# Up projection of a gated FFN: ScalarE writes the first product into the bank that the later ones add onto, two bank sums a pair, four buffers for products that run ahead

## The chip, the cores and the metric

The kernel runs on one core of one Trainium2 chip. The metric is the device time of one execution in microseconds; lower is better. Five engines work side by side, each through its own queue in a fixed order: TensorE (PE), VectorE (DVE), ScalarE (ACT), GpSimd (POOL) and SyncE (SP), which here issues the DMA transfers. PE writes its sums into banks of 128 x 512 float32 in PSUM; the other engines read them from there.

## The reference

One decoder layer on 1024 positions of 1024 channels: layer norm, a mixing sublayer (a convolution branch and a state-space branch), and a gated feed-forward block (FFN), each with a residual and a layer norm. The change lies in the FFN:

```python
u, g = split(h @ w_ffn_up)              # 1024 x 1024 times 1024 x 5632
u, g = causal depthwise conv of 3 taps along the positions, plus bias
y = (u * silu(g)) @ w_ffn_down          # 1024 x 2816 times 2816 x 1024
h = layer_norm(alpha * h + y)
```

(The names are shortened; the convolution runs over both halves.)

## The kernel before, in words

**Matmuls.** Each float32 operand is split into two parts of a shorter format, a high part (a cast on ACT) and what is left of it (a subtraction on DVE). `mm3` makes one product of three matmuls, high x high, high x low and low x high (L165, L166, L167). A *product* in the FFN is four `mm3` steps, 12 matmuls of 128 x 512, into one bank.

**Up projection.** 22 steps j; each makes 128 channels of the value half (`uv`) and 128 of the gate half (`ug`) for all 1024 positions. Positions and channels are cut into 2 x 2 blocks, and a scheme of Strassen's kind makes a step of seven products instead of eight. The position blocks and their sums are ready ahead: b11, b21, b22, t1, t2, t3, t4. `up_first` (L805) makes two products, b11 and b11 + b21, in one bank of the pool `pacc`; ACT copies the bank out after each (L811, L815), and the copy goes to DRAM (`first_scr`). The first 8 steps' `up_first` run ahead; the other 14 are spread over the 22 steps. `up_rest` (L837) makes the five others: `up_weights` loads two raw weight blocks (`ra`, `rb`), makes their sums on DVE (L828 to L831) and splits them (`split_pair`: cast L730, subtraction L731); `s` and half of `ug` come back from `first_scr`; and the products t2, t1, t3, b22 and t4 go into three banks of the pool `psm`, which has four. DVE takes the sums from the banks (L853, L855, L857, L859, L861):

```python
product(pb, lambda i: w24[:, i, :HALF], bl["t2"], True)
V.tensor_tensor(out=s, in0=s, in1=pb, op=ALU.add)                 # L853
product(pd, lambda i: w10[:, i, :HALF], bl["t1"], True)
V.tensor_tensor(out=uv[:, late], in0=s, in1=pd, op=ALU.add)       # L855
```

The convolution follows: one ACT pass with the third tap (L867) and two DVE passes (L871) for each half, silu on ACT (L881) and the gate on DVE (L882), tile `fo`. Every second step then makes sums of the two steps' results for the down projection (L896 to L899) and stores them to DRAM (`b_scr`, `t_scr`).

**Down projection.** `down` (L903) makes seven products p of 11 steps k, each with its own sum of weights and of stored blocks. `load(p, k)` fetches both halves into a tile `dr`, makes sums where p needs them (L924 for p=4, with a second tile `do`), and splits the tile into `w_dn` (L990, L991). Raw tiles come in turn from `wst` and from `raw` of the up projection, three buffers each; `w_dn` comes from two pools of three. For p=0 and p=1 `load` also fetches the blocks c3 and c4 (tile `c`, L955 and L959), which later products need. c4 and the rows of the last layer norm (`ln_g`, `ln_b`) lie where the position blocks of the up projection lay.

**Order.** A scheduler orders each engine's instructions when the kernel is built; `tc.high_priority` lets a block's instructions go as far ahead as buffers and data allow. SP's queue holds all loads and stores in one line.

Of the kernel before, what the change touches and what calls it, by code (L numbers as in the profile page):

```python
# [8 lines left out]
F32 = mybir.dt.float32  # L9
F32R = mybir.dt.float32r  # L10
AF = mybir.ActivationFunctionType
ALU = mybir.AluOpType
# [4 lines left out]
P = 128  # L17
D = 1024
# [37 lines left out]
def kernel(  # L56
# [30 lines left out]
    def bank(which):  # L87
# [53 lines left out]
    b2_scr, t32_scr, t41_scr = (  # L141
        [dram.tile([P, T], F32, name=f"{n}_scr{k}") for k in range(NK)] for n in ("b2", "t32", "t41")
    )
    c_scr = [dram.tile([8, P, HALF], F32, name=f"c_scr{i}") for i in range(2)]
    g_scr = [dram.tile([8, P, HALF], F32, name=f"g_scr{i}") for i in range(2)]
# [659 lines left out]
    def up_first(qp, bl, j):  # L805

        w = weights(wup[2 * j], f"ue{j}")
        ps = bank(1)
        product(ps, lambda i: w[:, i, 0:HALF], bl["b11"], True)
        s1 = qp.tile([P, HALF], F32, tag="first", bufs=2, name=f"s1_{j}")  # L810
        A.copy(s1, ps)  # L811
        SY.dma_start(first_scr[j][0], s1)
        product(ps, lambda i: w[:, i, HALF:D], bl["b21"], False)
        c11 = qp.tile([P, HALF], F32, tag="first", bufs=2, name=f"c11_{j}")
        A.copy(c11, ps)  # L815
        SY.dma_start(first_scr[j][1], c11)

    def up_weights(upp, j):


        with tc.high_priority(offset=2000):
            r1 = upp.tile([P, D], F32, tag="raw", bufs=3, name=f"ra{j}")
            SY.dma_start(r1, wup[2 * j])
            r2 = upp.tile([P, D], F32, tag="raw", bufs=3, name=f"rb{j}")
# [3 lines left out]
            V.tensor_tensor(out=s3, in0=a11, in1=a21, op=ALU.add)  # L828
            V.tensor_tensor(out=a21, in0=a21, in1=a22, op=ALU.add)
            V.tensor_tensor(out=a11, in0=a21, in1=a11, op=ALU.add)  # L830
            V.tensor_tensor(out=a12, in0=a12, in1=a11, op=ALU.add)  # L831
            w24 = split_pair(wsp, r1, f"s24_{j}")
            w10 = split_pair(wsp, r2, f"s10_{j}")
            w3 = split_pair(upp, s3, f"s3_{j}", HALF, 2)
        return w24, w10, w3

    def up_rest(upp, bl, j, before):  # L837

        w24, w10, w3 = up_weights(upp, j)
        ug, uv = (
            upp.tile([P, T + 32], F32, tag="u", bufs=3, name=f"f{n}{j}") for n in ("ug", "uv")
        )
        s = upp.tile([P, HALF], F32, tag="s", bufs=2, name=f"s{j}")
        SY.dma_start(s, first_scr[j][0])
        SY.dma_start(ug[:, 2 : 2 + HALF], first_scr[j][1])
        G.memset(ug[:, :2], 0.0)
        G.memset(uv[:, :2], 0.0)
        pb, pc_, pd = bank(0), bank(0), bank(0)  # L850
        late = slice(2 + HALF, 2 + T)
        product(pb, lambda i: w24[:, i, :HALF], bl["t2"], True)
        V.tensor_tensor(out=s, in0=s, in1=pb, op=ALU.add)  # L853
        product(pd, lambda i: w10[:, i, :HALF], bl["t1"], True)
        V.tensor_tensor(out=uv[:, late], in0=s, in1=pd, op=ALU.add)  # L855
# [3 lines left out]
        V.tensor_tensor(out=ug[:, late], in0=s, in1=pd, op=ALU.add)  # L859
        product(pc_, lambda i: w10[:, i, HALF:], bl["t4"], False)  # L860
        V.tensor_tensor(out=uv[:, 2 : 2 + HALF], in0=pc_, in1=s, op=ALU.subtract)  # L861
        os = []
        j = j // 2 + j % 2 * NK
        for jj, u in ((j, ug), (NF + j, uv)):
            o = upp.tile([P, T], F32, tag="o", bufs=3, name=f"fo{jj}")
            wc = PC_FW + 3 * jj
            A.activation(  # L867
                out=o, in_=u[:, 2 : 2 + T], func=AF.Identity, scale=pc[:, wc + 2 : wc + 3]
            )
            for k in range(2):  # L870
                V.scalar_tensor_tensor(  # L871
                    out=o,
                    in0=u[:, k : k + T],
                    scalar=pc[:, wc + k : wc + k + 1],
                    in1=o,
                    op0=ALU.mult,
                    op1=ALU.add,
                )
# [20 lines left out]
        V.tensor_tensor(out=a[:, early], in0=b[:, early], in1=t[:, late], op=ALU.add)  # L899
        SY.dma_start(t32_scr[j - NK], t)  # L900
        SY.dma_start(t41_scr[j - NK], a)

    def down(upp, dp, g, b):  # L903

# [18 lines left out]
        def add(dst, x, y):  # L923
            V.tensor_tensor(out=dst, in0=x, in1=y, op=ALU.add)  # L924
# [3 lines left out]
        def raw(name):  # L928
            nonlocal n_raw
            n_raw += 1  # L930
            pl, tag = ((wst, "st"), (upp, "raw"))[n_raw % 2]
            return pl.tile([P, D], F32, tag=tag, bufs=3, name=f"{name}_{n_raw}")

        last = []

        def load(p, k):
# [5 lines left out]
                b2_scr[k][:, E],  # L942
                t32_scr[k][:, L],
                t32_scr[k][:, E],
                t41_scr[k][:, L],
                t41_scr[k][:, E],
                b2_scr[k][:, L],
            )[p]
            with tc.high_priority(offset=4000):
                st = raw("dr")  # L950
                w_st = st[:, E]
                SY.dma_start(st[:, L], x)
                if p == 0:
                    SY.dma_start(w_st, a11)
                    SY.dma_start(c3[k], a21)  # L955
                    add(c3[k], c3[k], w_st)
                elif p == 1:
                    SY.dma_start(w_st, a12)
                    SY.dma_start(c4[k], a22)  # L959
                    add(c4[k], c4[k], w_st)  # L960
                elif p == 2:
                    SY.dma_start(w_st, a22)
                    add(w_st, w_st, c3[k])
                elif p == 3:
                    w_st = c3[k]
                    add(c4[k], c4[k], c3[k])
                elif p == 4:
                    other = raw("do")[:, E]
                    SY.dma_start(w_st, a21)
                    SY.dma_start(other, a22)  # L970
                    add(w_st, w_st, other)
                elif p == 5:
                    SY.dma_start(w_st, a22)
                else:
# [14 lines left out]
                for cs, src in cuts:  # L989
                    A.copy(w[:, 0, cs], src)  # L990
                    V.tensor_tensor(  # L991
                        out=w[:, 1, cs], in0=src, in1=w[:, 0, cs].bitcast(F32), op=ALU.subtract
                    )
            n_steps += 1
            return w

# [207 lines left out]
```

## Time and profile before

| | us |
|---|---|
| median of 3 runs | 2027.96 (2027.19 to 2028.29) |
| the profiled execution | 2030.96 |
| its span in the trace | 2029.3 |
| PE busy in it | 1973.4 |
| DVE busy | 1732.8 |
| ACT busy | 987.5 |

The mean granted clock of TensorE was 0.994. The up stage lies at about 1409 to 1804 us of the span and down from there to the end. A row of the trace has the start or a sum of busy time, the engine, the line of the kernel, out<-in with the program's names, partitions x elements, and in brackets the idle time before and who ended it. Lines of the profile before are those of the kernel before.

### The profile page before, as it was taken

The page shows a single profiled execution, that of the slowest core. Times are in us where ns is not written, and L with a number is a line of the kernel's source. Part 1 is how long each engine was busy: PE and PEld are TensorE (multiplying, and loading weights), DVE is VectorE, ACT ScalarE, POOL GpSimd, SP SyncE. Part 2 cuts the span into 40 slices and gives each one's busy share as a digit, 9 for nine tenths or more (in the row PEclk, how much of TensorE's full clock was granted, in tenths as well). Part 3 has the DMA queues.
Part 4 walks back from the last instruction along what each step waited for, and adds up shares of the span by engine and source line. Part 5 has one row for each costly group of instructions (what it writes and reads, how often), then busy time and mean ns, then how long its engine had stood idle before and what let it go on. Part 6 is the DMA issues. An engine that isn't in the chain of part 4 may idle for free. (4 is left out here: it accounts for less than half of the span.)

```text
span 2029.3 us, 24897 instructions
## 1 busy us (share of the span) xinstructions
PE 1973.4 (97%) x9164; PEld 1624.7 (80%) x9164; DVE 1732.8 (85%) x2307; ACT 987.5 (49%) x1403; POOL 147.1 (7%) x125
## 2 busy tenths in 40 slices
PE   7999999999999999999999999999999999989998
PEld 6888887888788888888888888887878788768886
DVE  7599999989766868999998976586899899889768
ACT  4465654556453265665454635364444344334432
POOL 2010101001400000100100121001000000000000
PEclk9999999999999999999999999999999999999999
DMA  6222233332545532222323254576545545578463
GB/s 219 94 64 93 80 102 106 98 105 99 166 126 194 214 104 73 89 83 84 115 89 117 96 171 129 169 252 223 166 161 199 169 161 197 184 292 279 161 226 109
DMA packets 109274, 297.14 MB, mean 146 GB/s; under 512 B 12384, under 2 KB 12384, under 8 KB 109152
## 3 DMA queue, kind: packets, MB, share of 16 engines
q1 hardware_dynamic: 109152, 295.55, 43.7%
q8 instruction: 72, 1.18, 0.2%
q14 instruction: 50, 0.41, 0.1%
HBM read 238.61 MB, written 56.89 MB: 146 GB/s over the span
## 5 line engine op out<-in xcount | busy, mean ns | idle before, releaser
L419 DVE SCALAR_TENSOR_TENSOR c<-v,pc,c 128x512 f32<-128x512 f32 x480 | 374.9, 804 | 8.4 <-ACT c L408 7.0
L477 POOL TENSOR_TENSOR au<-seg_mv,head_of 128x1024 fp32r<-128x1024 f32 x32 | 76.9, 2403 | 963.6 <-PE sm L486 730.1
L165 PE MATMUL acc<-hT,w_c 128*128 128x512 f32 x352 | 141.0, 401 | 0.0
L166 PE MATMUL acc<-hT,w_c 128*128 128x512 f32 x352 | 140.5, 399 | 0.0
L167 PE MATMUL acc<-hT,w_c 128*128 128x512 f32 x352 | 138.4, 393 | 0.0
L165 PE MATMUL sm<-h1s,w_s 128*128 128x512 f32 x264 | 104.6, 396 | 11.2 <-DVE fuv L855 9.1
L374 DVE SCALAR_TENSOR_TENSOR xbc<-u,pc,xbc 128x512 f32<-128x512 f32 x144 | 109.8, 775 | 0.7 <-ACT xbc L372 0.5
L990 ACT CAST w_dn<-dr 128x1024 fp32r<-128x1024 f32 (+1 forms) x73 | 68.7, 945 | 83.7 <-DVE dr L924 32.4
L166 PE MATMUL sm<-h1s,w_s 128*128 128x512 f32 x264 | 103.5, 392 | 0.0
L167 PE MATMUL sm<-h1s,w_s 128*128 128x512 f32 x264 | 102.8, 392 | 0.0
L166 PE MATMUL acc<-w_z,hT 128*128 128x512 f32 x256 | 100.8, 394 | 0.0
L165 PE MATMUL acc<-w_z,hT 128*128 128x512 f32 x256 | 100.8, 401 | 0.0
L167 PE MATMUL acc<-w_z,hT 128*128 128x512 f32 x256 | 100.7, 396 | 0.0
L153 ACT CAST w_c<-st_c 128x1024 fp32r<-128x1024 f32 x50 | 52.5, 1051 | 86.4 <-PE acc L167 65.6
L991 DVE TENSOR_TENSOR w_dn<-dr,w_dn 128x1024 fp32r<-128x1024 f32 (+1 forms) x73 | 78.9, 1089 | 11.2 <-ACT w_dn L990 11.1
L166 PEld LDWEIGHTS acc<-hT,w_c 128*128 128x128 f32 x352 | 66.1, 188 | 16.9 <-issue 3.8
L167 PEld LDWEIGHTS acc<-hT,w_c 128*128 128x128 f32 x352 | 66.1, 188 | 16.1 <-issue 2.6
L165 PEld LDWEIGHTS acc<-hT,w_c 128*128 128x128 f32 x352 | 66.1, 188 | 15.9 <-issue 2.6
L154 DVE TENSOR_TENSOR w_c<-st_c,w_c 128x1024 fp32r<-128x1024 f32 x47 | 60.6, 1289 | 20.3 <-ACT w_c L153 20.3
L165 PE MATMUL acc<-h1b,w_ue 128*128 128x512 f32 x176 | 70.0, 398 | 6.8 <-ACT s L811 6.8
L165 PEld LDWEIGHTS sm<-h1s,w_s 128*128 128x128 f32 x264 | 50.1, 190 | 25.9 <-DVE fuv L855 12.2
L166 PE MATMUL acc<-h1b,w_ue 128*128 128x512 f32 x176 | 69.5, 395 | 0.0
(336 smaller groups left out, 5723.1 us busy)
## 6 DMA issues: line engine op xcount, KB each, us to landing
st_c<-wcol SPq DMA_DIRECT2D x50, 512.0 KB, 3.6
st_z<-wz SPq DMA_DIRECT2D x32, 512.0 KB, 3.5
dr<-wdown SPq DMA_DIRECT2D x55, 256.0 KB, 4.5
st_wo<-wo SPq DMA_DIRECT2D x24, 512.0 KB, 4.0
st_ue<-wup SPq DMA_DIRECT2D x22, 512.0 KB, 3.8
ra<-wup SPq DMA_DIRECT2D x22, 512.0 KB, 3.6
rb<-wup SPq DMA_DIRECT2D x22, 512.0 KB, 3.9
t_scr<-fo SPq DMA_DIRECT2D x22, 512.0 KB, 3.5
```

Of the source, the lines that this page charges most:

```text
L153: A.copy(w[:, 0, :], st)
L154: (eng or V).tensor_tensor(out=w[:, 1, :], in0=st, in1=w[:, 0, :].bitcast(F32), op=ALU.subtract)
L165: TE.matmul(ps, wa(0), xa(0), start=start, stop=False, skip_group_check=more)
L166: TE.matmul(ps, wa(0), xa(1), start=False, stop=False, skip_group_check=more)
L167: TE.matmul(ps, wa(1), xa(0), start=False, stop=stop, skip_group_check=more)
L374: V.scalar_tensor_tensor(out=o, in0=u[:, k : k + HALF], scalar=pc[:, wc + k : wc + k + 1], in1=o, op0=ALU.mult, op1=ALU.add,)
L419: V.scalar_tensor_tensor(out=accs[i], in0=v[:, k : k + HALF], scalar=pc[:, wc + k : wc + k + 1], in1=accs[i], op0=ALU.mult, op1=ALU.add,)
L477: G.tensor_tensor(out=au, in0=seg_mv[:, c, :].unsqueeze(1).to_broadcast([P, 8, P]), in1=head_of[:, g, :].unsqueeze(2).to_broadcast([P, 8, P]),
L990: A.copy(w[:, 0, cs], src)
L991: V.tensor_tensor(out=w[:, 1, cs], in0=src, in1=w[:, 0, cs].bitcast(F32), op=ALU.subtract)
```

## The change

In `up_rest` two banks take the place of three. From step 2 on ACT copies `s` into a bank and t2 adds onto it; ACT copies the bank out to `s`; t1 adds onto the same bank and ACT copies it out to `uv`; b22 adds onto it and ACT copies it out to `ug`. t3 and t4 have the second bank, and DVE makes two sums from it. In steps 0 and 1 t2 starts its bank afresh and DVE adds `s`. The products are written in the order t2, t3, t1, t4, b22.

The rest makes room: the copies of `up_first` take turns in four buffers of the tag `first` instead of two; the raw weights come from two buffers in even steps and from `wst` in odd ones; the sum of L899 is no longer made and stored in the up stage, so `t41_scr` shrinks to `t1_scr`, and `load` makes it for p=5 from a second load (`t2`) and a sum. In `load` the fetches of c3 and c4 stand behind the weights' split and outside the high priority, the raw pool has two buffers instead of three, and `w_dn` takes its second pool from n_steps 3 on instead of 5.

```diff
@@ up_first
-        product(ps, lambda i: w[:, i, 0:HALF], bl["b11"], True)
-        s1 = qp.tile([P, HALF], F32, tag="first", bufs=2, name=f"s1_{j}")
-        A.copy(s1, ps)
-        SY.dma_start(first_scr[j][0], s1)
-        product(ps, lambda i: w[:, i, HALF:D], bl["b21"], False)
-        c11 = qp.tile([P, HALF], F32, tag="first", bufs=2, name=f"c11_{j}")
-        A.copy(c11, ps)
-        SY.dma_start(first_scr[j][1], c11)
+        for q, block in enumerate(("b11", "b21")):
+            product(ps, lambda i: w[:, i, q * HALF : (q + 1) * HALF], bl[block], q == 0)
+            f = qp.tile([P, HALF], F32, tag="first", bufs=4, name=f"first{q}_{j}")
+            A.copy(f, ps)
+            SY.dma_start(first_scr[j][q], f)
@@ up_weights
-            r1 = upp.tile([P, D], F32, tag="raw", bufs=3, name=f"ra{j}")
+            r1, r2 = (
+                wst.tile([P, D], F32, tag="st", name=f"r{n}{j}")
+                if j % 2
+                else upp.tile([P, D], F32, tag="raw", bufs=2, name=f"r{n}{j}")
+                for n in "ab"
+            )
...
@@ up_rest
-        pb, pc_, pd = bank(0), bank(0), bank(0)
-        late = slice(2 + HALF, 2 + T)
-        product(pb, lambda i: w24[:, i, :HALF], bl["t2"], True)
-        V.tensor_tensor(out=s, in0=s, in1=pb, op=ALU.add)
-        product(pd, lambda i: w10[:, i, :HALF], bl["t1"], True)
-        V.tensor_tensor(out=uv[:, late], in0=s, in1=pd, op=ALU.add)
-        product(pc_, lambda i: w3[:, i], bl["t3"], True)
-        V.tensor_tensor(out=uv[:, late], in0=pc_, in1=uv[:, late], op=ALU.subtract)
-        product(pd, lambda i: w24[:, i, HALF:], bl["b22"], False)
-        V.tensor_tensor(out=ug[:, late], in0=s, in1=pd, op=ALU.add)
-        product(pc_, lambda i: w10[:, i, HALF:], bl["t4"], False)
-        V.tensor_tensor(out=uv[:, 2 : 2 + HALF], in0=pc_, in1=s, op=ALU.subtract)
+        ps, pz = bank(0), bank(0)
+        early, late = slice(2, 2 + HALF), slice(2 + HALF, 2 + T)
+        seeded = j > 1
+        if seeded:
+            A.copy(ps, s)
+        product(ps, lambda i: w24[:, i, :HALF], bl["t2"], not seeded)
+        if not seeded:
+            V.tensor_tensor(out=ps, in0=s, in1=ps, op=ALU.add)
+        A.copy(s, ps)
+        product(pz, lambda i: w3[:, i], bl["t3"], True)
+        product(ps, lambda i: w10[:, i, :HALF], bl["t1"], False)
+        A.copy(uv[:, late], ps)
+        V.tensor_tensor(out=uv[:, late], in0=pz, in1=uv[:, late], op=ALU.subtract)
+        product(pz, lambda i: w10[:, i, HALF:], bl["t4"], False)
+        V.tensor_tensor(out=uv[:, early], in0=pz, in1=s, op=ALU.subtract)
+        product(ps, lambda i: w24[:, i, HALF:], bl["b22"], False)
+        A.copy(ug[:, late], ps)
...
-        V.tensor_tensor(out=a[:, early], in0=b[:, early], in1=t[:, late], op=ALU.add)
         SY.dma_start(t32_scr[j - NK], t)
-        SY.dma_start(t41_scr[j - NK], a)
+        SY.dma_start(t1_scr[j - NK], a[:, late])
@@ down, load
-            pl, tag = ((wst, "st"), (upp, "raw"))[n_raw % 2]
-            return pl.tile([P, D], F32, tag=tag, bufs=3, name=f"{name}_{n_raw}")
+            pl, tag, bufs = ((wst, "st", 3), (upp, "raw", 2))[n_raw % 2]
+            return pl.tile([P, D], F32, tag=tag, bufs=bufs, name=f"{name}_{n_raw}")
...
-                if p == 0:
-                    SY.dma_start(w_st, a11)
-                    SY.dma_start(c3[k], a21)
-                    add(c3[k], c3[k], w_st)
-                elif p == 1:
-                    SY.dma_start(w_st, a12)
-                    SY.dma_start(c4[k], a22)
-                    add(c4[k], c4[k], w_st)
+                if p < 2 or p == 5:
+                    SY.dma_start(w_st, (a11, a12, None, None, None, a22)[p])
+                if p == 5:
+                    t2 = raw("t2")[:, E]
+                    SY.dma_start(t2, t32_scr[k][:, L])
+                    add(st[:, L], st[:, L], t2)
...
-                    own = n_steps % 2 and n_steps > 4
+                    own = n_steps % 2 and n_steps > 2
...
+            if p < 2:
+                c = (c3, c4)[p][k]
+                SY.dma_start(c, (a21, a22)[p])
+                add(c, c, w_st)
```

How this moves instructions on the queues that the prediction speaks of is seen in two places. Line numbers after are those of the changed kernel. First ACT in steps 8 and 9 of the up stage, before (`w_s` are weight splits, `fo` convolution passes, `acc` a bank of `up_first`):

```order
L730 CAST w_s_8_12291<-ra_12282 128x1024
L867 ACTIVATE fo_12229<-fug_12154,pc 128x1024
L730 CAST w_s_8_12294<-rb_12284 128x1024
L815 COPY c_13_12279<-acc_12251 128x512
L881 ACTIVATE fo_12229<-fo_12229,pc 128x1024
L730 CAST w_s_9_12401<-s_9_12390 128x512
L867 ACTIVATE fo_12233<-fuv_12155,pc 128x1024
L730 CAST w_s_9_12395<-ra_12386 128x1024
```

And ACT there after (`sm_12303` and `sm_12407` are the banks of steps 8 and 9 that take t2, t1 and b22; L856 is the seed, L860, L863 and L868 the copies out):

```order
L860 COPY s_12298<-sm_12303 128x512
L856 COPY sm_12407<-s_12402 128x512
L888 ACTIVATE fo_12226<-fo_12226,pc 128x1024
L731 CAST w_s_10_12542<-s_10_12531 128x512
L863 COPY fuv_12297<-sm_12303 128x512
L860 COPY s_12402<-sm_12407 128x512
L731 CAST w_s_9_12394<-rb_12383 128x1024
L868 COPY fug_12296<-sm_12303 128x512
L874 ACTIVATE fo_12371<-fug_12296,pc 128x1024
```

The copies that free or fill PE's banks now stand among the casts and convolution passes of other steps: the copy to `s` of step 9, for instance, is ahead of the cast of that step's second weight block, and the copy to `uv` of step 8 is behind the cast of step 10's third.

Second, SP's queue at the passage into down, before (`dr` with `b_scr` and `wdown` is one step k of p=0: 14193 is k=4; `c_0` to `c_6` are c4, `c` x11 is c3):

```order
L954 DMA dr_14193<-wdown 128x512
L892 DMA b_scr_158<-fo_13951 128x512
L959 DMA c_0_14086<-wdown 128x512
L959 DMA c_1_14087<-wdown 128x512
L959 DMA c_2_14088<-wdown 128x512
L959 DMA c_3_14089<-wdown 128x512
L959 DMA c_4_14090<-wdown 128x512
L959 DMA c_5_14091<-wdown 128x512
L955 DMA c_14084<-wdown 128x512 x11
L959 DMA c_6_14092<-wdown 128x512
```

And after, where `dr_14202` is k=5 and `dr_14182` is k=4:

```order
L960 DMA dr_14202<-wdown 128x512
L899 DMA b_scr_158<-fo_13941 128x512
L203 DMA ln_g<-prow 128x1024
L203 DMA ln_b<-prow 128x1024
L998 DMA c_0_14075<-wdown 128x512
L998 DMA c_1_14076<-wdown 128x512
L998 DMA c_2_14077<-wdown 128x512
L998 DMA c_3_14078<-wdown 128x512
L998 DMA c_14073<-wdown 128x512 x11
L998 DMA c_4_14079<-wdown 128x512
L958 DMA dr_14182<-b_scr_152 128x512
L960 DMA dr_14182<-wdown 128x512
```

Before, k=0 to 5 stand ahead of the blocks c3 and c4; now k=0, 1, 2, 3 and 5 do, the rows of the layer norm stand ahead of c4, and k=4 behind sixteen blocks and the two rows.

More of the change, by code (lines that the diff above doesn't have):

```diff
@@ L140 @@
     b11_scr = [dram.tile([P, HALF], F32, name=f"b11_scr{k}") for k in range(NK)]
-    b2_scr, t32_scr, t41_scr = (
-        [dram.tile([P, T], F32, name=f"{n}_scr{k}") for k in range(NK)] for n in ("b2", "t32", "t41")
+    t1_scr = [dram.tile([P, HALF], F32, name=f"t1_scr{k}") for k in range(NK)]
+    b2_scr, t32_scr = (
+        [dram.tile([P, T], F32, name=f"{n}_scr{k}") for k in range(NK)] for n in ("b2", "t32")
     )
@@ L808, in up_first @@
         ps = bank(1)
-        product(ps, lambda i: w[:, i, 0:HALF], bl["b11"], True)
-        s1 = qp.tile([P, HALF], F32, tag="first", bufs=2, name=f"s1_{j}")
-        A.copy(s1, ps)
-        SY.dma_start(first_scr[j][0], s1)
-        product(ps, lambda i: w[:, i, HALF:D], bl["b21"], False)
-        c11 = qp.tile([P, HALF], F32, tag="first", bufs=2, name=f"c11_{j}")
-        A.copy(c11, ps)
-        SY.dma_start(first_scr[j][1], c11)
+        for q, block in enumerate(("b11", "b21")):
[3 more added lines that the diff above has]
+            SY.dma_start(first_scr[j][q], f)
     def up_weights(upp, j):
         with tc.high_priority(offset=2000):
-            r1 = upp.tile([P, D], F32, tag="raw", bufs=3, name=f"ra{j}")
+            r1, r2 = (
[4 more added lines that the diff above has]
+            )
             SY.dma_start(r1, wup[2 * j])
-            r2 = upp.tile([P, D], F32, tag="raw", bufs=3, name=f"rb{j}")
             SY.dma_start(r2, wup[2 * j + 1])
@@ L944, in load @@
                 t32_scr[k][:, E],
-                t41_scr[k][:, L],
-                t41_scr[k][:, E],
+                t1_scr[k],
+                b2_scr[k][:, E],
                 b2_scr[k][:, L],
@@ L971, in load @@
                     add(w_st, w_st, other)
-                elif p == 5:
-                    SY.dma_start(w_st, a22)
-                else:
+                elif p == 6:
                     w_st = c4[k]
```

## Prediction

> **What bounds the kernel now.** I read the page first, then the waits of the TensorE (PE), then a table of busy time by stage, then the timeline at each stall. The page:
>
> ```profile
> span 2029.3 us, 24897 instructions
> ...
> PE 1973.4 (97%) x9164; PEld 1624.7 (80%) x9164; DVE 1732.8 (85%) x2307; ACT 987.5 (49%) x1403; POOL 147.1 (7%) x125
> ```
>
> PE works 97% of the span; the change takes no matmul away. So it can only win what PE loses between matmuls, in the stages that it touches. PE's waits in the whole run (us in total, times, the longest), those of the up and down stages:
>
> ```profile
> PE sm L165 <- DVE fuv L855: 9.1, 6, 2.7
> PE acc L165 <- ACT s L811: 6.8, 4, 4.7
> PE acc L165 <- ACT w_dn L990: 4.5, 1, 4.5
> PE sm L165 <- ACT w_s L730: 2.1, 3, 1.1
> ```
>
> The first is a bank sum of VectorE (DVE) that the change removes. The busy table puts these into stages; its columns are the window, its length, busy time of PE, weight loads, DVE, ScalarE (ACT) and POOL, then the granted clock, the DMA share and GB/s:
>
> ```profile
> 1399.00:1409.00 10.00, 5.34 (x13) 4.18 (x14) 5.69 (x7) 3.78 (x5) 0.00 (x0) 0.66 0.76 277
> 1409.00:1804.00 395.00, 381.57 (x1659) 311.11 (x1658) 349.62 (x417) 159.87 (x173) 4.07 (x41) 1.00 0.54 181
> 1804.00:1820.00 16.00, 16.00 (x72) 13.05 (x70) 15.40 (x17) 7.25 (x7) 0.00 (x0) 1.00 0.91 317
> 1820.00:1832.00 12.00, 7.53 (x25) 5.56 (x25) 9.30 (x13) 5.25 (x5) 0.00 (x0) 0.86 1.05 393
> ```
>
> The second row is the up stage: 395.00 us, 13.4 of them with PE idle, DVE busy for 349.62 (89%), ACT for 159.87 (40%). One product of 12 matmuls lasts as long as from here to here:
>
> ```profile
> 1417.20 0.39 PE L165 MATMUL acc<-h1b,w_ue 128*128 128x512 f32 x1
> ...
> 1419.92 0.39 PE L165 MATMUL sm<-h1s,w_s 128*128 128x512 f32 x1
> ```
>
> That is 2.72 us, 0.2267 a matmul. The stage's 1659 matmuls would take 376.1 us; it loses 395.0 - 376.1 = 18.9 us, 13.4 idle and 5.5 in matmuls that ran slowly. One of the six stalls at L855 shows both (start, length, engine, line, out<-in, idle time before):
>
> ```profile
> 1613.93 0.39 PE L167 MATMUL sm<-h1s,w_s 128*128 128x512 f32 x1
> 1615.08 1.28 DVE L871 SCALAR_TENSOR_TENSOR fo<-fuv,pc,fo 128x1024 f32<-128x1024 f32 x1
> 1616.27 0.68 DVE L855 TENSOR_TENSOR fuv<-s,sm 128x512 f32<-128x512 f32 x1
> 1616.87 0.69 DVE L831 TENSOR_TENSOR ra<-ra 128x512 f32<-128x512 f32 x1
> 1617.01 0.61 PE L165 MATMUL sm<-h1s,w_s 128*128 128x512 f32 x1 [2.69 <-DVE fuv L855]
> ...
> 1620.77 0.39 PE L165 MATMUL sm<-h1s,w_s 128*128 128x512 f32 x1
> ```
>
> PE ended t1 at 1614.3. The sum that frees the bank for b22 stood in DVE's queue behind a convolution step, began at 1616.27, and PE stood for 2.69 us. Then nine matmuls took 1620.77 - 1617.01 = 3.76 us instead of 2.04: 1.7 more at a lower clock. So the stall cost 4.4.
>
> The Trainium skill (TensorE: Matmul & The Clock Gate, Part 1) has the clock halve only after an idle window of about 3.4 us; by it, none of this stage's gaps would slow PE, the 5.5 us would be hand-overs that stay, and the change could win only the idle part, for a sum of about -1.7 instead of the one below. The trace disagrees, for 2.69 us were enough, so I count the slow matmuls as part of the gaps.
>
> **Part by part.** *Bank sums.* The stage's groups in 1409 to 1800 (busy, mean ns | idle before, releaser):
>
> ```profile
> L855 DVE TENSOR_TENSOR fuv<-s,sm 128x512 f32<-128x512 f32 x22 | 15.0, 683 | 2.0 <-PE sm L167 1.9
> L828 DVE TENSOR_TENSOR s<-ra,rb 128x512 f32<-128x512 f32 x21 | 14.5, 690 | 13.9 <-DMA rb<-wup 12.8 <-DMA t_scr<-fo 1.0
> L899 DVE TENSOR_TENSOR fo<-fo,fo 128x512 f32<-128x512 f32 x10 | 6.9, 685 | 0.0
> L811 ACT COPY s<-acc 128x512 f32<-128x512 f32 x14 | 8.2, 587 | 71.4 <-PE acc L167 48.4 <-issue 23.0
> ```
>
> From start to start a DVE sum takes 0.60 (1616.27 to 1616.87). Three of five go in each of 22 steps, two come back in the unseeded steps 0 and 1, and L899 goes 11 times: 64 x 0.60 + 11 x 0.60 = 45 us off DVE. 349.6 - 45 = 305 us, 80% of a stage of 380. ACT gets three copies in each of 22 steps and 20 seeds, 86 x 0.587 = 50 us: 210, 55%. Neither is a bound by its amount; the joints decide. Per step, three copies stand between products of one bank: t2, copy s, t1, copy uv, b22, copy ug, and the seed ahead of t2. I laid the ACT, DVE and PE orders of steps 8 to 11 on one clock with these durations: another product (2.72) stands in each joint, and the copy (0.59 and its hand-overs) ends before it does; the tightest joint had 0.08 us left. An end at step 20 has no cover: t2, t1 and b22 follow one another. An exposed copy costs the last matmul's drain (0.39 - 0.23 = 0.16), the copy, the hand-overs and a slower first matmul, about 1.0. Two of them are 2.0, and 2.5 for joints that slip (an estimate, between 0 and 10, since the tightest has little to spare): 4.5 left of 18.9, **-14.4** (-18.9 to -6.4).
>
> *Raw staging* in two buffers of `raw` and, for odd steps, `st`. I take nothing: the load ends at DVE (L828 waited 12.8 us for rb in 21 steps, 0.6 each, hidden by DVE's other work before PE needs the weights). Bare, it would cost up to 22 x 0.6 = 13, about A's price below.
>
> *Four first buffers.* The stall before the stage:
>
> ```profile
> 1400.42 0.69 DVE L828 TENSOR_TENSOR s<-ra,rb 128x512 f32<-128x512 f32 x1 [6.87 <-DMA rb<-wup]
> ...
> 1401.15 0.62 ACT L730 CAST w_s<-s 128x512 fp32r<-128x512 f32 x1 [6.06 <-DVE s L828]
> 1402.41 0.59 ACT L815 COPY c<-acc 128x512 f32<-128x512 f32 x1 [0.64 <-DMA first_scr<-c]
> 1403.02 0.58 ACT L811 COPY s<-acc 128x512 f32<-128x512 f32 x1
> 1403.66 0.80 PE L165 MATMUL acc<-h1b,w_ue 128*128 128x512 f32 x1 [4.74 <-ACT s L811]
> ```
>
> PE waits for a copy that stands in ACT's queue behind a weight cast, and that cast waits through DVE for the load of rb. The new order has the cast ahead of the copy as before, so only the 0.64 us goes in which the copy waited for the store of an older `first` buffer: **-0.6** (-0.6 to 0).
>
> *Into down.* This is where the change pays. T is the end of b22 of step 21; c4 and the layer norm's rows lie where its operands were, and load from then on:
>
> ```profile
> 1803.88 0.69 DVE L859 TENSOR_TENSOR fug<-s,sm 128x512 f32<-128x512 f32 x1 [0.36 <-PE sm L167]
> ...
> 1803.88 2.70 SPq L959 DMA_DIRECT2D c<-wdown  x6
> 1806.68 7.85 SPq L955 DMA_DIRECT2D c<-wdown  x11
> ...
> 1817.28 0.33 SPq L952 DMA_DIRECT2D dr<-b_scr  x1
> 1817.66 0.42 SPq L954 DMA_DIRECT2D dr<-wdown  x1
> ...
> 1823.52 1.04 ACT L990 CAST w_dn<-dr 128x1024 fp32r<-128x1024 f32 x1 [10.87 <-DMA dr<-wdown]
> ...
> 1824.62 1.37 PE L165 MATMUL acc<-w_dn 128*128 128x512 f32 x4 [4.45 <-ACT w_dn L990]
> ```
>
> Before: with T at 1803.9 the first row of k=6 stands in SP's queue behind 20 loads of c3 and c4 (5120 KB), and its cast starts at T + 19.6. PE has t4 and k=1 to 5 to do, 6 x 2.72 = 16.3 us, then waits 4.45. After: two raw buffers instead of three hold one k fewer ahead (0, 1, 2, 3 and 5), and dn_0 and dn_1 now stand in the gaps of step 21, so PE has only t4, k=2 and k=3 after T: 8.2 us. The load of k=4 stands behind the two rows (512 KB each) and 16 loads of c3 and c4, 5120 KB again. I take its cast about 0.8 us earlier than k=6's, since the 512-KB rows take fewer issues, at T + 18.8, and PE at T + 20.0: it waits 11.8 instead of 4.45, **+7.3**. Ends: +2 if c3's loads run ahead of T, since c3 lies in a block of SBUF that is free by then; +9 if PE's clock comes back later after the longer gap.
>
> The Trainium skill (Perfetto Trace Analysis, the note on HBM above 100%) gives about 435 GB/s as what 16 DMA engines can move for one core; at that, the 5120 KB and the row of k=4 would land about 1.5 us sooner and the term would be +5.8. The trace shows 393 GB/s in the full window (1820 to 1832), so I keep +7.3.
>
> *Down, p=4 and p=5.* p=5 now makes its operand from two loads and a sum, as p=4 does, and both keep `dr` in the two-buffer pool. The page's issues (KB each, us to landing), and the sum's and the split's groups of p=4 (1908 to 1948):
>
> ```profile
> dr<-wdown SPq DMA_DIRECT2D x55, 256.0 KB, 4.5
> do<-wdown SPq DMA_DIRECT2D x11, 256.0 KB, 3.1
> L991 DVE TENSOR_TENSOR w_dn<-dr,w_dn 128x1024 fp32r<-128x1024 f32 (+1 forms) x13 | 14.2, 1096 | 0.3 <-ACT w_dn L990 0.3
> L990 ACT CAST w_dn<-dr 128x1024 fp32r<-128x1024 f32 (+1 forms) x14 | 13.4, 960 | 19.6 <-DVE dr L924 16.2 <-PE sm L167 3.4
> L924 DVE TENSOR_TENSOR dr<-dr,do 128x512 f32<-128x512 f32 x11 | 7.6, 691 | 12.2 <-DMA dr<-wdown 8.4 <-DMA do<-wdown 2.4 <-issue 1.1
> ```
>
> A buffer is held for landing, sum, cast and subtraction: 3.1 + 0.7 + 1.0 + 1.1 = 5.9 with hand-overs 6.0, or 7.3 with the page's 4.5. Two buffers give a step each 3.0 (3.65) us; PE eats one in 2.72. Over 22 steps PE gains 6.2 (20) on the loads; the lead of the six `w` tiles (one is being read, so at most 5 x 2.72 = 13.6; I take 12) cover that at 3.0 and leave 8 at 3.65. I take the nearer row, the loads without a neighbour: **+0.5** (0 to +8).
>
> **Sum:** -14.4 - 0.6 + 7.3 + 0.5 = -7.2 us, on the profiled 2030.96. That run lies 3.0 above the median of 2027.96; the difference is carried over to the median: **2020.8 us**.
>
> **Rivals.** *A. ACT's queue becomes the path (slower).* The copies stand in one queue with weight casts (1.04 us) and convolution steps that wait for DVE. For it: the start's stall above is just this, and the tightest joints have under 0.4 us. Against: ACT is at 55%, and my laying-out found cover. If one copy a step goes bare, 22 x 1.0 = 22 stand in place of 4.5: -7.2 + 17.5 = +10.3, 2038.3 us. It decides from (4.5 + 7.2) / 22 = 0.53 us exposed per step on.
> *B. Two raw buffers starve p=4 and p=5:* +8 in place of 0.5, +0.3, 2028.3 us. For it: the 4.5-us landings; against: PE's one wait for a cast of `w_dn` in all of before is the 4.5 us above, none in p=4.
> *C. No longer wait into down:* the loads of c3 run before T. -14.5, 2013.5 us. Against: SP's order puts them behind the rows that wait for T.
> *D. Clock.* If a bare copy a step also brought the lower clock as the 2.69 us did, 22 x (1.0 + 1.7) = 60 in place of 4.5: +48, 2076 us. The gap of 1.0 us it needs is well under the 2.69 seen. The Trainium skill (TensorE: Matmul & The Clock Gate, A second HAM failure mode: psum-queue depth-cycling) reports a kernel whose short idles between groups in changing banks kept the clock swinging; no run here shows that at such gaps.
>
> **How the numbers follow.** The forecast gets 0.43, A 0.27, B 0.17, C 0.10, D 0.03. About 0.2%, 4.1 us, can be told from no change: faster (forecast, C) 0.53, within it (B) 0.17, slower (A, D) 0.30. The forecast's own range is 2014 to 2027, from its unknown terms; with the rivals 2012.5 to 2038 leaves out half of A, D and the low end of C, under 2 in 10.
>
> **What would show it.** Right: no wait of PE for L855's successors, waits of PE for ACT copies (L860, L863, L868) of under 5 us in the up stage, which then lasts near 380 us; a wait of some 12 us for a cast of k=4 right after it; at most 1 us in p=4 and p=5; the stall of 4.7 at the start still there, slightly shorter. Wrong: over 12 us of waits for the copies in the up stage (A), several waits for `w_dn` in p=4 and p=5 (B), a wait into down that is no longer than 4.5 (C), or a granted clock under 0.95 throughout the stage (D).

## The result and the profile after

The changed kernel is slower: 2032.95 us (median of 15 runs, 2029.21 to 2036.64) against 2027.97 of the kernel before in the same rounds. The ratio is 1.0022 with an interval of 1.0014 to 1.0030, so about 3 to 6 us more, 0.22%. A gain of 7.2 us was forecast. The profiled execution after took 2034.61 us, its span 2032.8; before, 2030.96 and 2029.3.

The page of the changed kernel:

```profile
span 2032.8 us, 24888 instructions
...
PE 1974.6 (97%) x9164; PEld 1624.8 (80%) x9164; DVE 1696.9 (83%) x2243; ACT 1031.2 (51%) x1489; POOL 147.3 (7%) x125
```

DVE did 36 us less and ACT 44 us more, as the change meant. PE's waits in the whole run, those of the up and down stages:

```profile
PE acc L166 <- ACT w_dn L992: 12.1, 2, 11.4
PE acc L166 <- ACT first L813: 3.7, 1, 3.7
PE sm L167 <- DVE w_dn L993: 2.4, 2, 1.3
...
PE acc L167 <- DVE w_dn L993: 0.8, 1, 0.8
PE sm L166 <- ACT fuv L863: 0.8, 1, 0.8
PE sm L166 <- ACT w_dn L992: 0.7, 1, 0.7
PE sm L166 <- ACT s L860: 0.7, 1, 0.7
```

The copies (L860, L863) stop PE for 1.5 us in all, the passage into down for 11.4; both were forecast. New are the waits at L993 and the smaller one at L992, all in p=4 and p=5. The same stretch of the up stage before and after, from the table of busy time:

```profile
1409.00:1790.00 381.00, 367.79 (x1599) 299.84 (x1597) 337.48 (x405) 154.17 (x167) 3.97 (x40) 1.00 0.55 183
```

```profile
1409.00:1790.00 381.00, 379.57 (x1667) 312.12 (x1666) 305.82 (x341) 205.56 (x259) 4.09 (x41) 1.00 0.53 182
```

PE's idle time there fell from 13.2 to 1.4 us. The up stage was won; it was given back later. To see where, every run is cut at four points of PE's timeline: the first product of `up_rest`, the start of the wait at the passage, its end, and the last matmul. From the length of a product (2.72) follows what each stretch loses: 138 products of the up stage and, ahead of the wait, the d steps of down that run before it (6 with three raw buffers, 4 with two), then the other 77 - d steps.

| us | up stage loses | wait at the passage | rest of down loses | last matmul to end | span |
|---|---|---|---|---|---|
| before | 19.5 | 4.5 | 2.1 | 9.4 | 2029.3 |
| after | 3.7 | 11.4 | 11.6 | 12.9 | 2032.8 |
| e1 two banks alone | 20.6 | 4.1 | 3.1 | 9.0 | 2030.7 |
| e2 all but the banks | 2.2 | 11.9 | 13.6 | 12.7 | 2031.1 |
| e3 stored sum | 5.2 | 14.8 | 8.5 | 10.1 | 2029.1 |
| e4 dr in three buffers | 3.7 | 11.5 | 2.5 | 12.1 | 2022.6 |
| e5 staging alone | 1.9 | 7.6 | 2.1 | 9.5 | 2015.7 |
| e6 staging and banks | 4.2 | 8.4 | 2.8 | 9.1 | 2017.4 |
| e7 three raw buffers | 8.2 | 9.3 | 4.9 | 12.9 | 2028.2 |
| e8 staging undone | 19.6 | 9.3 | 2.6 | 12.8 | 2038.7 |
| e9 two raw before | 24.8 | 9.2 | 12.0 | 10.2 | 2050.0 |
| e11 sum in p=5 | 7.0 | 7.0 | 2.5 | 12.6 | 2022.7 |

After against before: start of the stage 0.5 earlier, -15.8, +6.9, +9.5, +3.5, together +3.6; the spans differ by 3.5. Of the 9.5 us that the rest of down loses more, 2.2 lie in p=4 and 6.9 in p=5, by the time of each 12 matmuls above 2.72; the other 0.4 are slower matmuls right behind the longer wait. (e10 has no single wait at the passage and is told below.)

### The profile page after: what moved, and what is told of

Same layout as the page of the kernel before. It is cut to its first block, busy times and chain, and to the rows that moved or that the text cites. A ratio compares the mean times of both kernels' runs of the same rounds, so it can differ in the third digit from the quotient of the medians.

```text
span 2032.8 us, 24888 instructions
## 1 busy us (share of the span) xinstructions
PE 1974.6 (97%) x9164; PEld 1624.8 (80%) x9164; DVE 1696.9 (83%) x2243; ACT 1031.2 (51%) x1489; POOL 147.3 (7%) x125
## 4 chain that ended last, share of the span: by engine, by line
PE 72%; DVE 19%; DMA 5%; issue 3%; ACT 1%; SPq 0%; DVEq 0%; ACTq 0%
PE acc L166 16%; PE acc L168 16%; PE acc L167 16%; DVE c L420 6%; PE sm L166 5%; PE sm L168 5%; PE sm L167 5%; DMA dr<-wdown 2%; PE sm L534 2%; PE acc L357 1%; DVE xbc L375 1%; DVE w_dn L993 1%; PE sm L515 1%; DMA st_wo<-wo 1%; DMA dr<-b_scr 1%
## 5 line engine op out<-in xcount | busy, mean ns | idle before, releaser
L992 ACT CAST w_dn<-dr 128x1024 fp32r<-128x1024 f32 (+1 forms) x73 | 68.4, 945 | 112.0 <-DVE dr L930 58.2
L993 DVE TENSOR_TENSOR w_dn<-dr,w_dn 128x1024 fp32r<-128x1024 f32 (+1 forms) x73 | 78.6, 1091 | 13.3 <-ACT w_dn L992 12.7
L166 PE MATMUL acc<-w_dn 128*128 128x512 f32 x160 | 58.5, 397 | 12.1 <-ACT w_dn L992 12.1
```

The source lines that it names most:

```text
L166: TE.matmul(ps, wa(0), xa(0), start=start, stop=False, skip_group_check=more)
L993: V.tensor_tensor(out=w[:, 1, cs], in0=src, in1=w[:, 0, cs].bitcast(F32), op=ALU.subtract)
```

## The experiments

The first four experiments ask which part won the up stage and which part lost it again.

**e1, two banks alone.** The kernel before with `up_rest` as changed:

```diff
-        pb, pc_, pd = bank(0), bank(0), bank(0)
+        ps, pz = bank(0), bank(0)
...
+        if seeded:
+            A.copy(ps, s)
...
```

> The kernel before with the two banks and the seeds of up_rest alone; buffers, staging, first products and down as before. Theory (the up stage won about 16 us, and the parts of the change in down gave it back: about 7 at the passage, 9 in p=4 and p=5, 3.5 behind the last matmul): about 2012 us (2009 to 2015), up stage near 379 us, PE waits at most 5 us at the passage into down and not at all in p=5, some 9.4 us from the last matmul to the end. Rival (the losses in down follow from the up stage itself, which ends sooner and leaves less time for loads): 2024 to 2033, with waits in p=5 and a long tail as in the changed kernel.

Measured: 2029.63 us, ratio 1.0009 (1.0001 to 1.0018). No gain at all. The two rows answer to those above: the busy table, and DVE's group that waits for the raw weights:

```profile
1409.00:1790.00 381.00, 368.03 (x1592) 297.52 (x1592) 300.27 (x341) 195.67 (x249) 4.02 (x40) 1.00 0.53 182
```

```profile
L828 DVE TENSOR_TENSOR s<-ra,rb 128x512 f32<-128x512 f32 x21 | 14.4, 687 | 13.7 <-DMA rb<-wup 13.7
```

DVE is 37 us less busy and PE's idle time is the same 13 us. It only has other names, the copies and the splits, by this kernel's waits of PE:

```profile
PE sm L165 <- ACT fuv L861: 3.8, 4, 2.9
PE sm L165 <- ACT w_s L730: 3.4, 3, 1.5
PE sm L165 <- ACT s L858: 3.2, 6, 0.7
PE sm L167 <- DVE w_s L731: 1.4, 2, 0.9
PE acc L167 <- DVE w_ue L154: 1.1, 3, 0.5
```

Both theories fell: the banks won nothing, and nothing was lost in down because of them (the last three columns are about as before, and there is no wait in p=5). The time lies in the rival's range, but not for the rival's reason.

**e2, all but the banks.** `up_first` and `up_rest` of before in the changed kernel.

```diff
-        ps, pz = bank(0), bank(0)
+        pb, pc_, pd = bank(0), bank(0), bank(0)
...
```

> The changed kernel with up_first's buffers and up_rest's five bank sums as before; the staging of raw weights, the operand of p=5 and the order of loads in down as changed. Theory: the losses in down are all there without the gain, 7 + 9 + 3.5 on before: about 2047 us (2041 to 2050). Rival (losses follow from the up stage): within 3 us of before, 2025 to 2031.

Measured: 2034.21 us, 1.0029 (1.0020 to 1.0038). Its losses in down are those of the changed kernel, as the theory had it, but the up stage is as good as after, with five bank sums on DVE, so the time lies 7 us below the expected range:

```profile
1409.00:1790.00 381.00, 379.74 (x1676) 314.11 (x1675) 345.08 (x407) 162.78 (x174) 4.11 (x41) 1.00 0.55 184
```

DVE is busy for 345 of 381 us, more than before, and PE hardly waits. So DVE's load was not what stopped PE. What e2 and the changed kernel share against e1 is the staging of the raw weights, `t1` in place of `t41`, and the changes in down. The times of e2 and of the changed kernel, 1.0029 and 1.0022 of before, have intervals that overlap: there, the two banks win nothing that can be told from noise, and cost nothing.

**e3, stored sum.** The sum of L899 is made in the up stage again:

```diff
+        V.tensor_tensor(out=a[:, early], in0=b[:, early], in1=t[:, late], op=ALU.add)
...
-                    t2 = raw("t2")[:, E]
-                    SY.dma_start(t2, t32_scr[k][:, L])
-                    add(st[:, L], st[:, L], t2)
...
```

> The changed kernel, but the sum for p=5 is made in the up stage and stored (t41), as before, and p=5 loads it. Theory: p=5 needs one load and no sum, PE's waits there (about 9 us) go, and with the last products on time the tail behind the last matmul is 9 to 10 us again: 2020 to 2022 us, the wait at the passage still 10 to 12 us. Rival (two raw buffers are too few in p=4 and p=5 whatever p=5 loads): 2029 to 2033, waits of 5 us or more stay.

Measured: 2030.85, 1.0013 (1.0005 to 1.0022). The tail is short again (10.1), but the rest of down still loses 8.5. Of that p=5 loses 0.4, as the theory had it, and p=4 loses 5.9: `dr` has two buffers there as well. The wait at the passage grew to 14.8; in this kernel's SP queue five more loads of c4 stand ahead of k=4. They do not explain it alone, since the same 21 blocks stand ahead in e2, where PE waits 11.9. The expected 2020 to 2022 was missed by 9, and the time is the rival's.

**e4, dr in three buffers.** From p=4 on the pools change places:

```diff
             with tc.high_priority(offset=4000):
+                n_raw += p == 4 and k == 0
                 st = raw("dr")
```

> The changed kernel with one edit: from p=4 on the turn of the raw pools is swapped, so dr, which is held through the split, has the three buffers of st, and the second operand, free after the sum, has the two of raw. Theory (the two buffers that hold dr starve p=4 and p=5): waits there fall from about 9 to under 2 us and the tail is short again: 2020 to 2023. Rival (the second load and the sum are too much for the DMA engines or for DVE in any buffers): 2030 to 2033, waits as in the changed kernel.

Measured: 2023.9, 0.9980 (0.9971 to 0.9989), about 8.5 us below the changed kernel by one line (0.9980 against 1.0022 of before). All waits of PE from 1409 us on, in this kernel:

```profile
PE acc L166 <- ACT w_dn L993: 11.5, 1, 11.5
PE sm L166 <- ACT fuv L863: 0.8, 1, 0.8
PE sm L166 <- ACT s L860: 0.7, 1, 0.7
```

The waits of p=4 and p=5 are gone, and these two products lose nothing, with the second load and the sum still there. So the two buffers that held `dr` were the cause, and not the bytes or DVE. One cycle of them is seen in the changed kernel's timeline:

```profile
1941.64 2.56 DVE L993 TENSOR_TENSOR w_dn<-dr,w_dn 128x1024 fp32r<-128x1024 f32 x2
...
1944.23 0.32 SPq L958 DMA_DIRECT2D dr<-b_scr  x1
...
1947.96 0.69 DVE L930 TENSOR_TENSOR dr<-dr,t 128x512 f32<-128x512 f32 x1
...
1949.12 2.36 DVE L993 TENSOR_TENSOR w_dn<-dr,w_dn 128x1024 fp32r<-128x1024 f32 x2 [0.47 <-ACT w_dn L992]
...
1951.51 0.32 SPq L958 DMA_DIRECT2D dr<-b_scr  x1
```

The second of two splits ends at 1944.2, the load into its buffer is issued at 1944.23, the sum comes at 1947.96, the split ends at 1951.48, and the next load is issued at 1951.51: 7.28 us a buffer, 3.64 a step, and PE eats a step in 2.72. The tail stayed long (12.1), against the expectation.

The next four ask whether the staging won the up stage.

**e5, staging alone.** The kernel before with

```diff
-            r1 = upp.tile([P, D], F32, tag="raw", bufs=3, name=f"ra{j}")
+            r1, r2 = (
+                wst.tile([P, D], F32, tag="st", name=f"r{n}{j}")
+                if j % 2
+                else upp.tile([P, D], F32, tag="raw", bufs=3, name=f"r{n}{j}")
+                for n in "ab"
+            )
...
```

> The kernel before with one edit: raw weights of odd steps come from st, those of even steps from raw, which keeps its three buffers; five bank sums on DVE and down as before. First theory (two banks and seeds won the up stage): no gain there, 2026 to 2031 us, PE waits for L855 of about 9 us stay. New theory (the 19 us were lost because DVE waited for the load of rb, and the raw buffers decide when that load starts): the up stage loses under 6 us instead of 19.5, no waits for L855, some -14 us, 2013 to 2018 us if the passage into down stays at 4.5.

Measured: 2015.46 us, 0.9934 (0.9921 to 0.9946), the fastest kernel here with e10, and in the expected range, though the wait at the passage is 7.6 and not 4.5. Its busy table and its group of L832 (L828 of before):

```profile
1409.00:1790.00 381.00, 379.58 (x1674) 313.93 (x1674) 349.83 (x415) 161.01 (x174) 4.07 (x41) 1.00 0.55 189
```

```profile
L832 DVE TENSOR_TENSOR s<-ra,rb 128x512 f32<-128x512 f32 x20 | 13.7, 687 | 3.0 <-DMA rb<-wup 2.9
```

DVE's wait for rb fell from 12.8 to 2.9 us and PE's idle time from 13.2 to 1.4, with DVE at 92%. The waits themselves (us in total, times, the longest), before and then in e5:

```profile
DVE s L828 <- DMA rb<-wup: 12.8, 10, 3.0
```

```profile
DVE s L832 <- DMA rb<-wup: 2.9, 4, 1.2
```

Before, five of the six sums of L855 that kept PE waiting start 2 to 9 us after such a wait ended. How early the weights are there can be read from the time between DVE's first sum of a step's raw weights and PE's first product of the same step in `up_rest` (median of steps 3 to 20). It is 17.2 us before, 13.3 in e1, 13.1 in e8 and 12.9 in e9, the four kernels whose up stage loses 19.5 us or more. In the kernels with the staging, which lose 1.9 to 8.2, it is 23.6 to 30.3.

**e6, staging and banks.** e5 with `up_rest` as in e1.

> The staging edit of e5 and the two banks with seeds, all else as before. First theory (both add up, banks the larger part): 2010 us or below. New theory: the banks have nothing left to win once the loads are early: within 4 us of e5, 2010 to 2018 us, ACT about 50 us busier and DVE 38 us less busy with no effect on PE.

Measured: 2021.18, 0.9961 (0.9949 to 0.9974): 5.7 above e5 by the medians of the same rounds, more than the 4 allowed for. In the two profiles it is 3.4 from the start of the stage on (2.3 in the up stage, 0.8 at the passage, 0.7 in down, -0.4 in the tail); the profiled executions, 2019.07 and 2017.46 us, lie closer together than the medians, so the profiles hold only part of the 5.7. Here the banks do not only win nothing, they cost. What DVE gained it waits for, by the waits of DVE in 1409 to 1790, before, after the change, and in e6:

```profile
DVE w_s L731 <- ACT w_s L730: 7.0, 12, 1.3
```

```profile
DVE w_s L732 <- ACT w_s L731: 45.1, 25, 3.3
```

```profile
DVE w_s L731 <- ACT w_s L730: 43.2, 21, 4.7
```

The subtraction of a split now waits for a cast that stands in ACT's queue among the copies: 38 us more after than before, about what the removed sums had taken (36 by the page), and 40 more in e6 than in e5, which has 3.3.

**e7, three raw buffers** (and two `first` buffers) in the changed kernel:

```diff
-                else upp.tile([P, D], F32, tag="raw", bufs=2, name=f"r{n}{j}")
+                else upp.tile([P, D], F32, tag="raw", bufs=3, name=f"r{n}{j}")
...
-            pl, tag, bufs = ((wst, "st", 3), (upp, "raw", 2))[n_raw % 2]
+            pl, tag, bufs = ((wst, "st", 3), (upp, "raw", 3))[n_raw % 2]
```

> The changed kernel with three raw buffers in place of two, in the up stage and in down, and two first buffers instead of four (there is no room for both). Theory: the passage holds k=0 to 5 ahead again, so PE has 5.4 us more to do and waits 5 to 8 us instead of 11.4; dr has three buffers in p=4 and p=5, so the waits there fall from 9 to under 3 and the tail is short: 2015 to 2020 us. Rival (the rows of the layer norm ahead of c4, not the buffers, make the passage long): wait of 10 to 12 us, 2022 to 2025.

Measured: 2028.0, 0.9990 (0.9982 to 0.9999), 8 above the expected range. The rest of down loses 4.9 instead of 11.6, and nothing of it in p=4 and p=5. But the up stage loses 8.2, at its end, where PE waits for weights of down that are put earlier in its queue, and the wait is 9.3 and the tail 12.9. Three raw buffers mend p=4 and p=5 and not the passage, where the rows of the layer norm and the blocks stand ahead of k=6 just as well; the expectation was right in the first and wrong in the second, in the tail and in the time.

**e8, staging undone** in the changed kernel: e7 with all raw weights from `raw`.

> The changed kernel with all raw weights from raw again, three buffers, two first buffers; two banks, seeds, stored t1 and down as changed. New theory (staging won the up stage): the gain goes, the up stage loses 17 to 22 us as in e1; with three buffers in down the passage and p=5 cost little, so 2028 to 2036. First theory (banks won it): the up stage loses under 6 us and the time is 2015 to 2020.

Measured: 2039.35, 1.0048 (1.0034 to 1.0061), 11 above e7 in the same rounds; the time is above the expected range, and the up stage loses 19.6, as expected. With e1 and e5 this makes all four cells: without the staging the stage loses 19.5 (old banks) or 20.6 and 19.6 (new banks); with it 1.9 to 7.0 (old banks: e5, e2, e11) or 3.7 to 8.2 (new banks: after, e3, e4, e6, e7).

The last three try the size of that effect, the passage and the tail.

**e9, two raw buffers** in the kernel before (`bufs=3` to `bufs=2` for `raw`).

> The kernel before with two raw buffers in place of three, nothing else. Theory (the number of raw weight tiles that can be in flight sets the loss of the up stage: 3 lose 19.5 us, 5 or 6 lose 2 to 5): the loss grows to 30 us or more, waits of DVE for rb above 14 us; and the passage into down waits 10 to 12 instead of 4.5: 2043 to 2065 us. Rival (three already are as good as two, it is the place of the tiles that matters): up stage as before, 2030 to 2040.

Measured: 2048.2, 1.0090 (1.0076 to 1.0104). The time is in the range, and the up stage loses 24.8: more than with three, less than the 30 expected. DVE's wait for rb was not longer than before (9.4 us against 12.8), so that row alone does not measure what too few buffers cost; here the sums that free the banks came late more often (L855 stopped PE nine times instead of six). The wait at the passage rose from 4.5 to 9.2, less than the 10 to 12 expected. The rest of down loses 12.0, of it 5.6 in p=4, where `dr` has two buffers as in e3, and 4.5 at a wait for weights in p=1.

**e10, paced blocks.** e5, and a block of c3 or c4 is loaded only when the weights of its step are split:

```diff
+            if p < 2:
+                c = (c3, c4)[p][k]
+                G.tensor_copy(c[:, :1], w[:, 1, :1].bitcast(F32))
+                SY.dma_start(c, (a21, a22)[p])
+                add(c, c, w_st)
...
```

> The staging edit of e5, and in down the load of each block of c3 and c4 made to wait for the split of the weights of its own step (a copy of one column by GpSimd from the split into the block goes ahead of the load), so that they no longer stand in one block ahead of k=6. Theory (the wait at the passage is the time of the 20 loads ahead of k=6 in SP's queue): the wait falls from 7.6 to under 3 us: 2009 to 2013 us. Rival (all those bytes must come in anyway and the wait only moves to a later step): 2014 to 2018, with waits for w_dn later in p=0 and p=1.

Measured: 2016.86, 0.9934 (0.9921 to 0.9947), the same as e5. The wait of 7.6 at the passage is gone, and seven shorter ones take its place between 1790 and 1866 us, 8.0 in all; the two longest:

```profile
1850.26 0.50 PE L166 MATMUL acc<-w_dn 128*128 128x512 f32 x1 [1.77 <-DVE w_dn L991]
...
1865.52 0.50 PE L166 MATMUL acc<-w_dn 128*128 128x512 f32 x1 [2.36 <-DVE w_dn L991]
```

The rival was right: the blocks' loads ahead of k=6 set where PE waits, not how long.

**e11, sum in p=5.** e5 with the operand of p=5 made in down, as in the changed kernel:

```diff
+                    t2 = raw("t2")[:, E]
+                    SY.dma_start(t2, t32_scr[k][:, L])
+                    add(st[:, L], st[:, L], t2)
...
```

> The staging edit of e5, and the sum for p=5 made in down from two loads, as in the changed kernel; three raw buffers. Theory (the tail is DVE's backlog: it is full in the last 40 us, and the sums of p=5 push weight splits into them): PE waits in p=5 under 2 us, but 12 to 13 us from the last matmul to the end instead of 9.5: some 3 us above e5, 2017 to 2020. Rival (the long tail comes from p=5 running late): tail 9 to 10 us, within 1 us of e5.

Measured: 2024.04, 0.9973 (0.9963 to 0.9983), so 8.6 above e5's 2015.46, measured in other rounds (7.9 by the ratios), and 4 above the expected range. PE does not wait in p=5 (rest of down 2.5) and the tail is 12.6 all the same. So a late p=5 is not what makes the tail long; making the sum in down does it. All thirteen kernels divide by it: in the seven that store the sum in the up stage the tail is 9.0 to 10.2 us, in the six that make it in down 12.1 to 12.9. In the last 40 us before the last matmul DVE is busy for 35.3 to 38.2 us in every kernel; what it does in them, before and then after the change:

```profile
L229 DVE SCALAR_TENSOR_TENSOR rows<-rows,rs_f,ln_b 128x512 f32<-128x512 f32 x12 | 8.3, 742 | 0.0
...
L991 DVE TENSOR_TENSOR w_dn<-dr,w_dn 128x512 fp32r<-128x512 f32 x6 | 4.1, 683 | 0.0
```

```profile
L993 DVE TENSOR_TENSOR w_dn<-dr,w_dn 128x512 fp32r<-128x512 f32 (+1 forms) x10 | 8.4, 847 | 2.5 <-ACT w_dn L992 2.5
...
L230 DVE SCALAR_TENSOR_TENSOR rows<-rows,rs_f,ln_b 128x512 f32<-128x512 f32 x8 | 5.4, 739 | 0.0
```

Splits that were done earlier before (4.3 us of them) fall into these 40 us, four passes of the layer norm (2.9) fall out behind the last matmul, and the end moves by 3.5. In the seven kernels with the stored sum DVE makes 15 splits in these 40 us, in the six others 18 to 21. That e11 lost 5 us more in the up stage than e5 (7.0 against 1.9) is not explained; one sum a pair less stands there, and its two waits for L860 (4.1 us) are new.

## Why the prediction was wrong

The forecast was 7.2 us less; the medians moved by 5.0 the other way. Two terms carried the difference: p=4 and p=5, put at +0.5, took about 9, and the tail, which the sum leaves out, took 3.5. The up stage came out near its forecast size for another reason than the one given. Of the signs that were named for being right only one failed: PE waited 4.6 us in p=4 and p=5 instead of at most 1. That is also the sign that was named for rival B.

- **p=4 and p=5, +0.5.** Measured about +9 (2.2 in p=4, 6.9 in p=5). This step set the direction of the result. It is rival B's mechanism, and B priced it at 8. The time for which a buffer is held was mis-sized. The prediction took 3.1 us, "the nearer row", for the landing and 6.0 in all. In the cycle shown under e4 both halves of the operand are there 4.3 us after the first load is issued, the split stands behind that of another step, and the buffer is held for 7.28, the upper end that the prediction gave (7.3). At 3.64 us a step against PE's 2.72 the lead of the `w` tiles was used up before p=4 ended. e4 shows the cause by taking it away.
- **Up stage, -14.4.** Measured -15.8, for a reason that the prediction priced at nothing, so that the size is luck. It read the stalls at L855 as a sum that stands behind other work in DVE's queue, which is so, and gave the gain to the banks that take sums off DVE. e1 and e6 show that the banks win nothing, e5 that the staging wins it all. The step that failed is the one on raw staging, put at nothing because "the load ends at DVE (L828 waited 12.8 us for rb in 21 steps, 0.6 each, hidden by DVE's other work before PE needs the weights)". These were ten waits of up to 3.0 us, not 21 of 0.6, and five of the six stalls at L855 follow one of them. With DVE 89% busy there was little time to make them good. The row that carried the stage was quoted and set aside. That the staging is the cause is shown; that it works through the earlier load is what DVE's waits and the leads given under e5 say, though in e9 the wait for rb alone did not grow with the loss.
- **Clock.** The forecast counted 5.5 us of slow matmuls as part of the gaps, against the rule of the Trainium skill (TensorE: Matmul & The Clock Gate, Part 1). Nearly all of them went with the gaps: the stage lost 3.7 instead of 19.5, where that rule, as the prediction applied it, would have left at least 5.5. But only one of the stage's twelve gaps, the one of 2.69 us, shows a lower clock, worth 1.7 us. The rest comes with every gap: the end of the matmul ahead of it (0.39 - 0.23 = 0.16 us) and a slower first one behind it (0.34 instead of 0.23). Rival D asked whether many short gaps lower the clock: e1 has 17 gaps of up to 1.5 us in the up stage beside its one of 2.93, and a granted clock of 1.00 there.
- **Copies in ACT's queue (rival A).** The places of the copies held: 1.5 us of waits in the up stage against the 4.5 allowed for. What ACT's fuller queue cost went to DVE (45.1 us of waits for casts), which had time to spare then.
- **First buffers, -0.6.** The wait at the start fell from 4.74 to 3.73, and the stage began 0.5 earlier. No run shows that the buffers did it: e2, with two of them, waited 3.3, and e4, with four, 2.8.
- **Passage, +7.3.** Measured +6.9 in the wait (4.45 to 11.36), and in the way described. The rows of the layer norm are issued at 1790.26 us, right behind T; PE had 8.1 us of work from there and went on 19.5 after it, where the prediction has 8.2 and 20.0. Either part of the cause alone makes about two thirds of it: two raw buffers in the old order wait 9.2 (e9), the new order with three raw buffers 9.3 (e7, e8). The staging alone makes 7.6 (e5). No run takes the two rows away, and e10 shows, in e5, that moving the blocks moves the wait without shortening it.
- **The tail, not in the sum.** +3.5. DVE is busy for 36.3 of the last 40 us of before, and the change moves eleven sums and the splits behind them toward that stretch: 21 splits instead of 15. The prediction looked at what PE waits for and not at the engine that ends the kernel.

With B's size in place of the forecast's, the sum of the prediction is about 2028 us; the tail makes the rest of the way to a slower kernel.

## What to carry to other kernels

When PE waits for a sum on a busy engine, ask first what that engine itself waited for: 13 us of DVE's waits at one load explained more here than 36 us of its work did. A pool shared by a new consumer is priced by the time that one tile is held (7.3 us here) over the number of tiles, against what the consumer eats (2.72 a step), and the tile that is held longest belongs in the larger pool. When a change brings several edits that make room for one another, try the smallest alone: one of them, a different pool for every second pair of raw tiles, with `raw` left at three buffers, makes the kernel before 0.66% faster (2015.46 us, 0.9934, 0.9921 to 0.9946), and with the two banks added to it (e6) 5.7 us of that are lost again.

## What the runs showed of the hardware

The length of a gap alone did not decide here whether TensorE's clock fell. Gaps of 2.69 us before and of 2.93 in e1 brought half rate (0.43 us a matmul in place of 0.23) at once, and one of 2.37 before did not. In e9 a gap of 1.94 brought it and a longer one, of 2.27, did not. The first two matmuls after each, 0.63 us long at half rate and 0.39 at full rate:

```profile
1511.60 0.74 PE L165 MATMUL sm<-h1s,w_s 128*128 128x512 f32 x1 [1.94 <-DVE fuv L855]
1512.13 0.63 PE L166 MATMUL sm<-h1s,w_s 128*128 128x512 f32 x1
...
1622.65 0.50 PE L165 MATMUL sm<-h1s,w_s 128*128 128x512 f32 x1 [2.27 <-DVE fuv L855]
1622.98 0.39 PE L166 MATMUL sm<-h1s,w_s 128*128 128x512 f32 x1
```

In e11 the first matmuls after a gap of 3.24 ran at full rate, and half rate began 0.8 us later:

```profile
1786.52 0.50 PE L166 MATMUL sm<-h1s,w_s 128*128 128x512 f32 x1 [3.24 <-DVE fuv L860]
...
1787.32 0.59 PE L166 MATMUL sm<-h1s,w_s 128*128 128x512 f32 x1
1787.71 0.63 PE L167 MATMUL sm<-h1s,w_s 128*128 128x512 f32 x1
```

In e10 it began 1.3 us after the end of the gap of 2.36 shown above. So the clock follows a gap at a time of its own. The Trainium skill (TensorE: Matmul & The Clock Gate, Part 1) describes a window of about 3.4 us that runs free of the kernel. The delayed start fits that; the gaps of 1.94, 2.69 and 2.93, shorter than the whole window which it asks for, do not.
